# Delta rule: inverse blocks merged by 32x32 products, key lengths from Gram diagonals, decay rows spread through DRAM

## The chip, the cores and the metric

One Trainium2 chip, of which the kernel uses one core. The metric is the device time of one execution in microseconds (us), lower is better. Engines are named as in the profile: PE is TensorE, DVE is VectorE, ACT is ScalarE, POOL is GpSimd; SP is the engine on whose queue all transfers of this kernel are issued (SPq in the profile's rows).

## The reference

A decoder of four layers, each a sequence mixer and an MLP, and a further block behind them, over 16 meta tokens and 256 tokens (T = 272 columns), width 1024, all in float32. Layers 0 and 3 have a gated delta rule as mixer, which is what the change touches. Cut to that:

```python
def gated_deltanet(u, valid, w_in, conv_w, a_log, dt_bias, norm_w, w_out):
    proj = u @ w_in                                   # q, k, v, z, beta, a
    qkv = silu(causal_depthwise_conv(proj[..., :DN_CONV_CH], conv_w))
    q = l2norm(q) * DN_HEAD_K ** -0.5;  k = l2norm(k)  # 8 heads of 128
    beta = sigmoid(beta_logit);  g = -exp(a_log) * softplus(a + dt_bias) * m
    o = chunk_gated_delta_rule(q, k, v, beta, g)
    return (rmsnorm(o, norm_w) * silu(z)) @ w_out

def chunk_gated_delta_rule(q, k, v, beta, g):         # per chunk and head
    gc = cumsum(g)
    decay = exp(where(incl, gc[:, None] - gc[None, :], -inf))
    a_strict = where(strict, (k * beta) @ k.T * decay, 0)
    m = a_strict + eye                                # unit lower triangular
    u = triangular_solve(m, v * beta);  w = triangular_solve(m, k * beta * exp(gc))
    # scan over chunks: v_new = u - w @ state; o = (q*exp(gc)) @ state + (q @ k.T * decay) @ v_new
```

## The kernel before

The residual stream stays on the chip as 128 partitions by 8 by T. Weights come from DRAM in chunks of 1 MB: `chunk` (L405 to L416) issues one load on SP into `wraw` (three buffers), splits it into a high part `whi` (ACT cast, two pieces of 128x1024) and a low part `wlo` (DVE subtraction, four pieces of 128x512, three buffers each). Every product with weights (`mm3`) is three PE products, high by high, high by low and low by high; they show as `pm`. The stages follow one another: delta rule layer 0 (`dn0`, about 6 to 215 us), its MLP, an attention layer, MLP, a recurrent layer, MLP, delta rule layer 3 (`dn3`, about 1050 to 1245 us), and a last block.

In a delta rule layer `_dn` walks through 16 weight chunks in the order k0 k1 v0 q0 k2 v1 q1 k3 z0 v2 q2 v3 q3 z1 z2 z3, each for one pair of heads (four pairs) and each 48 PE products. The load of the next chunk is asked for when the current one begins. The work of the delta rule itself is written as generators that are advanced between the products (`tick`, every 8 products), so it lies in the gaps of the weight products in PE's row of work. A scheduler then fixes one order for each engine and each queue by its own cost model, and each engine works through its list strictly in that order: an instruction that waits holds all behind it, and a transfer on SP that waits for its source or its buffer holds every later load.

The generators that the change touches:
- `dn_gate_cols` (L650 to L702) works out the running sums of the gates and lays them as rows, one of 272 columns per head: PE writes `grow` (8x272), ACT copies it to `rows` in SBUF (L702).
- `dn_ssq` (L742) gives squared lengths of 272 columns for a pair: an ACT square of 128x544 (`sq`), six one-column PE products with ones (`ssq`), a DVE memset and a DVE addition. It is called for the keys (by `dn_keys`) and for the queries (by `dn_chain`).
- `dn_keys` (L755), per pair: for each head PE spreads its row of `rows` over 128 partitions by a product with columns of the identity (`pg`, in PSUM); ACT takes its exponential (`E`, 128x272 per head); DVE subtracts the gate columns under a mask from it (`Dx` 128x128 four times, `Dm` 16x16 twice), ACT exponentiates these. Then key lengths (`kk`, `sk`, `sv`), the Gram products `ga` (four 128x128) and `gm` (two 16x16), and from them DVE forms the triangular matrices `U`.
- `dn_blocks` (L921) inverts all 16x16 diagonal blocks of `U` at once: `U` is written to DRAM (`ud`), read back as 40 blocks (`X`), POOL does the 15 steps, and the result goes through DRAM again (`yd`, `yc`). These four transfers are on SP, between the weight loads, and `yd` waits for POOL.
- `dn_merge` (L947) joins blocks of 16 to blocks of 32, 64 and 128. The step to 32 uses masked full-width operands: DVE builds `uw`, `yf` and `gf` (each 128x512, eight block-diagonal copies under masks), PE does four products of 128x128 by 32 columns for `gp` and eight for `pp`. The later steps use products of single quadrants, 32x32 and 64x64.
- `dn_chain` (L807) runs the recurrence of a pair and needs the list `keys` full and the pair before it solved. Its `kp` products turn the keys and values of the meta tokens.

In the trace each float32 PE product of the delta rule shows as two MATMUL instructions, a transpose as one.

Of the kernel before, what the change touches and what calls it, by code (L numbers as in the profile page):

```python
# [9 lines left out]
F32 = mybir.dt.float32  # L10
F32R = mybir.dt.float32r
AF = mybir.ActivationFunctionType
ALU = mybir.AluOpType
# [127 lines left out]
def _dn_consts():  # L141
    p = np.arange(P)[:, None]
    q = np.arange(P)[None]
    c = np.arange(32)[None]
    comp = (p % 32 >= 16) & (c < 16)
    full = np.concatenate([comp & (p // 32 == b) for b in range(4)], axis=1)
    r = [("mc16", comp), ("mf16", full),
         ("bm32", p // 32 == q // 32), ("in16", p // 16 == np.arange(8)[None]), ("in32", p // 32 == np.arange(4)[None]),
         ("hf16", (p // 16) % 2 == np.arange(2)[None]), ("hf32", (p // 32) % 2 == np.arange(2)[None]),
         ("st16", p % 32 == np.arange(16)[None]), ("mneg", np.where(q >= p, 0.0, -1e30))]  # L150
    return [(n, np.asarray(a, np.float32)) for n, a in r]
# [148 lines left out]
class Prog:  # L300
# [89 lines left out]
    def mm(self, out, lhsT, rhs, start=True, stop=True):  # L390
        self.PE.matmul(out=out, lhsT=lhsT, rhs=rhs, start=start, stop=stop)  # L391
# [238 lines left out]
    def dn_gates(self, s, u, R):  # L630

        d1 = self.d1
        gates = [d1.tile([8, T], F32, name="rows")] + [d1.tile([P, 4, 5], F32, name=n) for n in ("bet", "gc", "ng")]
# [12 lines left out]
    def dn_gate_cols(self, s, gp, R, rows, bet, gc, ng):  # L646
# [55 lines left out]
        self.S.copy(out=rows, in_=rp)  # L702
# [52 lines left out]
    def dn_keys(self, p, kT, gates, ready, keys):  # L755
# [12 lines left out]
        keys += [E, Dx, Dm, sk, sv]  # L768
        for h in range(2):
            pg = self.pst("pg")[:, 0:T]  # L770
            r = 2 * p + h
            mm(pg, self.ident[0:8, r:r + 1].broadcast_to([8, P]), rows)
            act(E[:, h, :], pg, AF.Exp)
            for c in range(2):
                stt(Dx[:, 2 * h + c, :], pg[:, ck[1 + c]], gc[:, p, 2 * h + c:2 * h + c + 1], mneg, ALU.subtract, ALU.min)
            r = RH[h]
            stt(Dm[r], pg[r, 0:16], gc[r, p, 4:5], mneg[0:16, 0:16], ALU.subtract, ALU.min)
# [3 lines left out]
        yield  # L781
        self.dn_ssq(kT, kk)
        act(sk, kk, AF.Sqrt)
        V.reciprocal(out=sv, in_=kk)
        tt(sv, sv, bet[:, p, :], ALU.mult)
# [9 lines left out]
        for h in range(2):  # L795
            mm(gm[RH[h], 0:16], kT[:, h, 0:16], kT[:, h, 0:16])
        for i in range(4):
            stt(U[:, i, :], ga[:, i, :], sv[:, i:i + 1], Dx[:, i, :], ALU.mult, ALU.mult)
# [8 lines left out]
    def dn_chain(self, p, kT, vT, qT, gates, keys, outs, last):  # L807
# [41 lines left out]
        for h in range(2):  # L849
            r = RH[h]  # L850
            self.tr(kp[:, h, :], kT[:, h, ck[1]])
            mm(kp[r, 2, :], kT[:, h, 0:16], self.ident)
            mm(kp[r, 3, :], vT[:, h, 0:16], self.ident)
# [94 lines left out]
    def dn_merge(self, U, yc, Y):  # L948
# [13 lines left out]
        uw = d2.tile([P, 4, P], F32, tag="gf", name="uw", bufs=1)  # L962
        tt(uw, U[:, 0:4, :], bc(dc("bm32"), 1, 4), ALU.mult)
        Ym = d2.tile([48, 48], F32, tag="Ym", name="Ym")
        blocks(Ym.unsqueeze(1), yc[0:48, 4:5, 0, :], dc("in16")[0:48, 0:3], 16, 48, 1)
        yf = d2.tile([P, 4, P], F32, tag="yf16", name="yf", bufs=1)
        blocks(yf, yc[:, 0:4, 0, :], dc("in16"), 16)
# [4 lines left out]
        gp = self.pst("gp")[:, 0:128].rearrange("p (m a) -> p m a", m=4)  # L972
        for m in range(4):
            mm(gp[:, m, :], uw[:, m, :], yw[:, m, 1, :])
        gf = d2.tile([P, 4, P], F32, tag="gf", name="gf", bufs=1)
        gcm = d2.tile([P, 4, 32], F32, tag="gs", name="gcm", bufs=1)
        tt(gf.rearrange("p m (b a) -> p m b a", b=4), bc(gp, 2, 4), bc(dc("mf16").rearrange("p (b a) -> p b a", b=4), 1, 4), ALU.mult)
# [3 lines left out]
        for m in range(4):  # L981
            mm(pp[:, m, 0, :], gf[:, m, :], yw[:, m, 0, :])
            mm(pp[:, m, 1, :], yf[:, m, :], gcm[:, m, :])
# [900 lines left out]
```

## Time and profile before

| | |
|---|---|
| time, median of 3 runs | 2632.33 us |
| runs | 2615.8, 2632.33, 2635.84 us |
| the profiled execution | 2633.17 us |
| its span | 2631.0 us |
| PE busy | 2590.7 us, 98% |
| DVE busy | 2058.9 us, 78% |
| ACT busy | 1474.1 us, 56% |
| POOL busy | 109.5 us, 4% |

The span is what the trace covers; the time of the same execution is 2.17 us longer. The busy shares are means over all stages. The granted clock of PE is given as a part of its full 2.4 GHz, so 0.50 is 1.2 GHz.

### The profile page before, as it was taken

To read this page: it belongs to the slowest core of one execution; us is meant where nothing else is said; L and a number is where in the kernel's file an instruction comes from. 1 tells how busy PE (TensorE), PEld (TensorE's weight loads), DVE (VectorE), ACT (ScalarE), POOL (GpSimd) and SP (SyncE) were. 2 spreads that over 40 slices of the span, in tenths; PEclk is the share of its full clock that TensorE was granted. 3 is DMA by queue.
4 is the path that set the end of the run, shared out by engine and by line. 5 is a ranking of instruction groups with operands and counts; after the bars stand their busy time and mean duration, and the time that the engine had idled before them with its cause. 6 is when DMAs were issued, how large, how long until landed. Compare 5 with 4: busy or idle time off the path is not lost.

```text
span 2631.0 us, 51989 instructions
## 1 busy us (share of the span) xinstructions
PE 2590.7 (98%) x20890; PEld 2512.0 (95%) x20890; DVE 2058.9 (78%) x4637; ACT 1474.1 (56%) x2544; POOL 109.5 (4%) x280
## 2 busy tenths in 40 slices
PE   8999999999999999999999999999999999999998
PEld 8899999899999999989999999999788999999998
DVE  7768967679879976877986877976654987997765
ACT  7777445564457644877645545544544445445544
POOL 1410001000000000330000000000000000000000
PEclk9999999999999999999999999999997999999999
DMA  5226755247545664333875665654213875874553
GB/s 186 95 89 237 276 179 181 99 169 261 194 147 188 259 233 172 98 113 127 313 268 192 241 230 179 217 183 163 81 65 120 286 278 184 312 277 163 177 179 111
DMA packets 89570, 494.56 MB, mean 188 GB/s; under 512 B 18449, under 2 KB 28337, under 8 KB 33265
## 3 DMA queue, kind: packets, MB, share of 16 engines
q1 hardware_dynamic: 89328, 491.23, 53.0%
q8 instruction: 165, 2.70, 0.4%
q14 instruction: 77, 0.62, 0.1%
HBM read 485.23 MB, written 5.96 MB: 187 GB/s over the span
## 4 chain that ended last, share of the span: by engine, by line
PE 92%; DVE 4%; ACT 2%; POOL 1%; issue 1%; DMA 1%; SPq 0%; DVEq 0%; ACTq 0%; POOLq 0%
PE pm L391 81%; PE o L391 1%; PE sp L391 1%; PE ssq L391 1%; PE pp L391 1%; PE go L391 1%; PE ga L391 1%; DVE wlo L415 1%; PE gp L391 1%; PE po L391 1%; POOL yb L938 0%; ACT L358 0%; POOL t L937 0%; ACT whi L412 0%; ACT s L358 0%
## 5 line engine op out<-in xcount | busy, mean ns | idle before, releaser
L391 PE MATMUL pm<-uh,whi 128*128 128x258 f32 (+2 forms) x3768 | 1083.8, 288 | 5.6 <-ACT uh L358 4.0
L391 PE MATMUL pm<-uh,wlo 128*128 128x258 f32 (+2 forms) x3768 | 1086.3, 289 | 0.8 <-DVE wlo L415 0.8
L391 PE MATMUL pm<-ul,whi 128*128 128x258 f32 (+2 forms) x3768 | 1086.2, 289 | 0.3 <-DVE ul L352 0.2
L412 ACT CAST whi<-wraw 128x1024 fp32r<-128x1024 f32 (+1 forms) x767 | 768.4, 1033 | 533.1 <-PE pm L391 306.3
L415 DVE TENSOR_TENSOR wlo<-wraw,whi 128x512 fp32r<-128x512 f32 x1511 | 979.7, 688 | 94.9 <-ACT whi L412 92.4
L391 PEld LDWEIGHTS pm<-uh,whi 128*128 128x128 f32 x3768 | 717.6, 191 | 11.8 <-ACT uh L358 4.4
L391 PEld LDWEIGHTS pm<-uh,wlo 128*128 128x128 f32 x3768 | 717.7, 191 | 8.0 <-issue 4.2
L391 PEld LDWEIGHTS pm<-ul,whi 128*128 128x128 f32 x3768 | 718.0, 191 | 6.4 <-issue 4.2
L391 PE MATMUL pm<-hh,wlo 128*128 128x256 f32 (+1 forms) x1904 | 541.5, 284 | 0.0
L391 PE MATMUL pm<-hh,whi 128*128 128x256 f32 (+1 forms) x1904 | 541.4, 284 | 0.0
L391 PE MATMUL pm<-hl,whi 128*128 128x256 f32 (+1 forms) x1904 | 540.4, 284 | 0.0
L391 PEld LDWEIGHTS pm<-hl,whi 128*128 128x128 f32 x1904 | 361.2, 190 | 0.0
L391 PEld LDWEIGHTS pm<-hh,wlo 128*128 128x128 f32 x1904 | 358.7, 188 | 0.0
L391 PEld LDWEIGHTS pm<-hh,whi 128*128 128x128 f32 x1904 | 358.1, 188 | 0.0
L1375 DVE SCALAR_TENSOR_TENSOR wmod<-wmod,crow 128x1024 f32<-128x1024 f32 x144 | 174.4, 1216 | 0.1
L355 DVE TENSOR_TENSOR h<-h,pm 128x272 f32<-128x272 f32 (+1 forms) x192 | 82.1, 429 | 83.8 <-PE pm L391 83.2
L402 ACT CAST hh<-t 128x256 fp32r<-128x256 f32 x110 | 44.5, 405 | 146.2 <-DVE t L352 146.0
L358 ACT ACT_TABLE_LOAD x90 | 115.5, 1283 | 10.1 <-PE pm L391 4.1
L358 ACT ACTIVATE s<-r 128x272 f32<-128x272 f32 (+1 forms) x128 | 53.7, 425 | 71.1 <-DVE r L352 69.8
L358 ACT ACTIVATE t<-t,b 128x256 f32<-128x256 f32 x110 | 55.5, 506 | 64.0 <-DVE t L355 63.9
L355 DVE TENSOR_TENSOR t<-pm,rstd 128x256 f32<-128x256 f32 x220 | 90.7, 414 | 0.0
L352 DVE SCALAR_TENSOR_TENSOR h<-pm,gate,h 128x256 f32<-128x256 f32 x96 | 46.2, 481 | 50.1 <-PE pm L391 50.0
(456 smaller groups left out, 2847.1 us busy)
## 6 DMA issues: line engine op xcount, KB each, us to landing
wraw<-mlp SPq DMA_DIRECT2D x128, 1024.0 KB, 4.8
wmod<-wmod SPq DMA_DIRECT2D x72, 1024.0 KB, 6.2
wraw<-f1i SPq DMA_DIRECT2D x66, 1024.0 KB, 4.9
wraw<-f2i SPq DMA_DIRECT2D x44, 1024.0 KB, 5.0
wraw<-dnA SPq DMA_DIRECT2D x32, 1024.0 KB, 5.0
wraw<-f1o SPq DMA_DIRECT2D x24, 1024.0 KB, 4.9
wraw<-f2o SPq DMA_DIRECT2D x16, 1024.0 KB, 4.9
wraw<-daA SPq DMA_DIRECT2D x12, 1024.0 KB, 4.9
```

The costliest lines, as they stand in the source:

```text
L352: self.V.scalar_tensor_tensor(out=out, in0=a, scalar=s, in1=b, op0=op0, op1=op1)
L355: self.V.tensor_tensor(out=out, in0=a, in1=b, op=op)
L358: i = self.S.activation(out=out, in_=a, func=func, **k).ins
L391: self.PE.matmul(out=out, lhsT=lhsT, rhs=rhs, start=start, stop=stop)
L402: self.S.copy(out=hi, in_=x)
L412: self.S.copy(out=hi[:, k], in_=raw[:, k])
L415: self.V.tensor_sub(out=lo[:, k], in0=raw[:, k], in1=hi[:, k].bitcast(F32))
L1375: i = self.V.scalar_tensor_tensor(out=junk, in0=w[:, k, :], scalar=1.0, in1=c[:, r, :], op0=ALU.mult, op1=ALU.mult, accum_out=m[:, j:j + 1])
```

## The change

There are three parts, all in the delta rule, so all done for eight pairs of heads in the program (four in each of two layers).

1. `dn_merge`, the step from 16 to 32: `uw`, `yf` and `gf` are no longer built. `gp` is sixteen products of 32x32 on the diagonal quadrants of `U` and `yw`, `pp` is 32 products of 32x32 of `gcm` and `yw`. The constant `mf16` goes.
2. Key lengths: `dn_ssq` is no longer called for keys. DVE multiplies `ga` (four 128x128) and `gm` (two 16x16) by the identity and accumulates along the rows into `kk`. `sk`, `sv` and the list `keys` are therefore filled after the Gram products.
3. Decay rows: ACT copies `grow` to `rs` in SBUF, and a transfer takes it to `rows`, now in DRAM (L703). Per pair one transfer reads two rows into `E` on all 128 partitions (L769; 128x544 float32 is 278 KB); DVE forms `Dx` and `Dm` from `E` in SBUF, and then ACT exponentiates `E` in place, once. The `pg` products go.

Beside these, in `kp` of the first head of a pair, two products with the identity become transposes.

```diff
--- before.py
+++ after.py
@@ -143,8 +143,7 @@
     q = np.arange(P)[None]
     c = np.arange(32)[None]
     comp = (p % 32 >= 16) & (c < 16)
-    full = np.concatenate([comp & (p // 32 == b) for b in range(4)], axis=1)
-    r = [("mc16", comp), ("mf16", full),
+    r = [("mc16", comp),
          ("bm32", p // 32 == q // 32), ("in16", p // 16 == np.arange(8)[None]), ("in32", p // 32 == np.arange(4)[None]),
          ("hf16", (p // 16) % 2 == np.arange(2)[None]), ("hf32", (p // 32) % 2 == np.arange(2)[None]),
          ("st16", p % 32 == np.arange(16)[None]), ("mneg", np.where(q >= p, 0.0, -1e30))]
@@ -630,7 +629,7 @@
     def dn_gates(self, s, u, R):
 
         d1 = self.d1
-        gates = [d1.tile([8, T], F32, name="rows")] + [d1.tile([P, 4, 5], F32, name=n) for n in ("bet", "gc", "ng")]
+        gates = [self.dd.tile([8, T], F32, name="rows")] + [d1.tile([P, 4, 5], F32, name=n) for n in ("bet", "gc", "ng")]
         gw = self.gw if s == 0 else self.chunk(self.A[f"dng{s}"], 512)
         gp = self.pst("gates")
         n = 0
@@ -699,7 +698,9 @@
         for c in range(2):
             o, n = CB[1 + c]
             mm(rp[:, o:o + n], cs[:, 8 * c:8 * c + 8], self.ident)
-        self.S.copy(out=rows, in_=rp)
+        rs = d2.tile([8, T], F32, tag="rr", name="rs", bufs=1)
+        self.S.copy(out=rs, in_=rp)
+        self.nc.sync.dma_start(out=rows, in_=rs)
 
     def proj_out(self, name, ys, N, waits, add):
 
@@ -765,24 +766,17 @@
         Dx = d2.tile([P, 4, P], F32, tag="Dx", name="Dx")
         Dm = d2.tile([48, 16], F32, tag="Dm", name="Dm")
         kk, sk, sv = (d2.tile([P, 5], F32, tag=n, name=n, bufs=4) for n in ("kk", "sk", "sv"))
-        keys += [E, Dx, Dm, sk, sv]
+        self.nc.sync.dma_start(out=E, in_=bass.AP(rows.tensor, rows.offset + 2 * p * T, [[0, P], [1, 2 * T]]))
+        yield 3
         for h in range(2):
-            pg = self.pst("pg")[:, 0:T]
-            r = 2 * p + h
-            mm(pg, self.ident[0:8, r:r + 1].broadcast_to([8, P]), rows)
-            act(E[:, h, :], pg, AF.Exp)
             for c in range(2):
-                stt(Dx[:, 2 * h + c, :], pg[:, ck[1 + c]], gc[:, p, 2 * h + c:2 * h + c + 1], mneg, ALU.subtract, ALU.min)
+                stt(Dx[:, 2 * h + c, :], E[:, h, ck[1 + c]], gc[:, p, 2 * h + c:2 * h + c + 1], mneg, ALU.subtract, ALU.min)
             r = RH[h]
-            stt(Dm[r], pg[r, 0:16], gc[r, p, 4:5], mneg[0:16, 0:16], ALU.subtract, ALU.min)
+            stt(Dm[r], E[r, h, 0:16], gc[r, p, 4:5], mneg[r.start:r.start + 16, r.start:r.start + 16], ALU.subtract, ALU.min)
+        act(E, E, AF.Exp)
         act(Dx, Dx, AF.Exp)
         for r in RH:
             act(Dm[r], Dm[r], AF.Exp)
-        yield
-        self.dn_ssq(kT, kk)
-        act(sk, kk, AF.Sqrt)
-        V.reciprocal(out=sv, in_=kk)
-        tt(sv, sv, bet[:, p, :], ALU.mult)
         yield
         while p > 1 and self.inv[p - 2] is None:
             yield
@@ -794,6 +788,20 @@
             mm(ga[:, 2 * h + c, :], k, k)
         for h in range(2):
             mm(gm[RH[h], 0:16], kT[:, h, 0:16], kT[:, h, 0:16])
+
+        V.memset(kk, 0.0)
+        diag = d2.tile([P, P], F32, tag="dg", name="dg", bufs=1)
+        for i in range(4):
+            V.scalar_tensor_tensor(out=diag, in0=ga[:, i, :], scalar=1.0, in1=self.ident, op0=ALU.mult, op1=ALU.mult,
+                                   accum_out=kk[:, i:i + 1])
+        for r in RH:
+            V.scalar_tensor_tensor(out=diag[r, 0:16], in0=gm[r, 0:16], scalar=1.0, in1=self.ident[r, r], op0=ALU.mult,
+                                   op1=ALU.mult, accum_out=kk[r, 4:5])
+        V.tensor_scalar_add(out=kk, in0=kk, scalar1=EPS)
+        act(sk, kk, AF.Sqrt)
+        V.reciprocal(out=sv, in_=kk)
+        tt(sv, sv, bet[:, p, :], ALU.mult)
+        keys += [E, Dx, Dm, sk, sv]
         for i in range(4):
             stt(U[:, i, :], ga[:, i, :], sv[:, i:i + 1], Dx[:, i, :], ALU.mult, ALU.mult)
         for r in RH:
@@ -849,8 +857,11 @@
         for h in range(2):
             r = RH[h]
             self.tr(kp[:, h, :], kT[:, h, ck[1]])
-            mm(kp[r, 2, :], kT[:, h, 0:16], self.ident)
-            mm(kp[r, 3, :], vT[:, h, 0:16], self.ident)
+            for i, x in ((2, kT), (3, vT)):
+                if h:
+                    mm(kp[r, i, :], x[:, h, 0:16], self.ident)
+                else:
+                    self.tr(kp[r, i, :], x[:, h, 0:16])
         for h in range(2):
             r = RH[h]
             act(ke[:, h, :], kp[:, h, :], AF.Copy, scale=Dx[:, 2 * h, P - 1:P])
@@ -959,28 +970,26 @@
             nb = out.shape[-1] // w
             tt(out.rearrange("p m (b a) -> p m b a", b=nb), bc(y, 2, nb), bc(bc(mask, 1, m), 3, w), ALU.mult)
 
-        uw = d2.tile([P, 4, P], F32, tag="gf", name="uw", bufs=1)
-        tt(uw, U[:, 0:4, :], bc(dc("bm32"), 1, 4), ALU.mult)
         Ym = d2.tile([48, 48], F32, tag="Ym", name="Ym")
         blocks(Ym.unsqueeze(1), yc[0:48, 4:5, 0, :], dc("in16")[0:48, 0:3], 16, 48, 1)
-        yf = d2.tile([P, 4, P], F32, tag="yf16", name="yf", bufs=1)
-        blocks(yf, yc[:, 0:4, 0, :], dc("in16"), 16)
         yw = d2.tile([P, 4, 2, 32], F32, tag="yw", name="yw", bufs=1)
         for t in range(2):
             blocks(yw[:, :, t, :], yc[:, 0:4, t, :], dc("hf16"), 16)
         yield
         gp = self.pst("gp")[:, 0:128].rearrange("p (m a) -> p m a", m=4)
+        b32 = [slice(32 * b, 32 * b + 32) for b in range(4)]
         for m in range(4):
-            mm(gp[:, m, :], uw[:, m, :], yw[:, m, 1, :])
-        gf = d2.tile([P, 4, P], F32, tag="gf", name="gf", bufs=1)
+            for b in b32:
+                mm(gp[b, m, :], U[b, m, b], yw[b, m, 1, :])
         gcm = d2.tile([P, 4, 32], F32, tag="gs", name="gcm", bufs=1)
-        tt(gf.rearrange("p m (b a) -> p m b a", b=4), bc(gp, 2, 4), bc(dc("mf16").rearrange("p (b a) -> p b a", b=4), 1, 4), ALU.mult)
         tt(gcm, gp, bc(dc("mc16"), 1, 4), ALU.mult)
         yield
         pp = self.pst("pp")[:, 0:256].rearrange("p (m t a) -> p m t a", m=4, t=2)
         for m in range(4):
-            mm(pp[:, m, 0, :], gf[:, m, :], yw[:, m, 0, :])
-            mm(pp[:, m, 1, :], yf[:, m, :], gcm[:, m, :])
+            for b in b32:
+                mm(pp[b, m, 0, :], gcm[b, m, :], yw[b, m, 0, :])
+            for b in b32:
+                mm(pp[b, m, 1, :], yw[b, m, 0, :], gcm[b, m, :])
         tt(yw, yw, pp, ALU.subtract)
         blocks(Y, yw[:, :, 0, :], dc("in32"), 32)
         yt = d2.tile([64, 4, 64], F32, tag="yt", name="yt", bufs=1)
```

Counted over the program's instructions: `pg` 16 products to 0, one-column `ssq` products 96 to 48 for the delta rule, products of 128x128 by 32 columns 96 to 0, products of 32x32 in these two steps 0 to 384; DVE `uw`, `yf`, `gf` 8 each to 0, DVE products for `kk` 0 to 48; ACT `E` 16 of 272 columns to 8 of 544, squares of keys 8 to 0; SP gains two transfers for `rows` and eight for `E`.

The order also moves. First SP's queue in layer 0, from the load of chunk k2 on. `wraw<-dnA` are the weight loads, in order k2, v1, q1, k3 and so on; what stands in brackets is what the row waits for. Before:

```order
L409 DMA wraw<-dnA 128x2048 [waits DMAHW2_49,DMAHW5_49,DVE_49,Activation_49]
L409 DMA wraw<-dnA 128x2048 [waits DMAHW3_49,DMAHW6_49,DVE_49,Activation_49]
L409 DMA wraw<-dnA 128x2048 [waits DMAHW4_49,DVE_49,Activation_49]
L925 DMA ud<-U_201 128x5x128 [waits DMAHW0_49,DVE_49]
L927 DMA X<-ud 40x16x16 [waits DMAHW0_49,PE_49]
L925 DMA ud<-U_210 128x5x128 [waits DVE_49]
L409 DMA wraw<-dnA 128x2048 [waits DMAHW5_49,DVE_49,Activation_49]
L927 DMA X<-ud 40x16x16 [waits DMAHW2_49,DMAHW1_49,Pool_49]
```

The first three are the loads of v1, q1 and k3, the fourth is z0. After, the same stretch:

```order
L408 DMA wraw<-dnA 128x2048 [waits DMAHW2_49,DMAHW5_49,DVE_49,Activation_49]
L703 DMA rows<-rs 8x272 [waits DMAHW6_49,Activation_49]
L408 DMA wraw<-dnA 128x2048 [waits DMAHW3_49,DVE_49]
L769 DMA E<-rows 128x544 [waits DMAHW6_49,DMAHW0_49]
L769 DMA E<-rows 128x544
L936 DMA ud<-U_201 128x5x128 [waits DVE_49]
L938 DMA X<-ud 40x16x16 [waits DMAHW2_49,PE_49]
L408 DMA wraw<-dnA 128x2048 [waits DMAHW4_49,DVE_49]
L936 DMA ud<-U_210 128x5x128 [waits DMAHW5_49,DVE_49]
L938 DMA X<-ud 40x16x16 [waits DMAHW5_49,DMAHW3_49,Pool_49]
L953 DMA yd<-yb 40x512 [waits Pool_49]
L408 DMA wraw<-dnA 128x2048 [waits DMAHW0_49,DVE_49,Activation_49]
```

The loads here are v1, q1, k3 and z0: k3 has moved behind `ud` and `X` of pair 0, and z0 behind those of pair 1 and `yd` of pair 0.

Second, DVE's list at the same place, around the low parts of chunk k2 and `U` of pair 0 (`U_201`). Before:

```order
L355 TENSOR_TENSOR sv<-sv,bet 128x5
L553 MEMSET raw 128x3
L355 TENSOR_TENSOR raw<-pm,rstd 128x272
L415 TENSOR_TENSOR wlo<-wraw,whi 128x512 x4
L352 SCALAR_TENSOR_TENSOR U_201<-ga,sv,Dx 128x128 x4
L352 SCALAR_TENSOR_TENSOR U_201<-gm,sv,Dm 16x16 x2
L745 MEMSET ssq_527 128x1
L415 TENSOR_TENSOR wlo<-wraw,whi 128x512 x2
```

All four pieces of k2's low part stand ahead of `U` of pair 0. After (the first two pieces stand further up, ahead of all `Dx`):

```order
L351 SCALAR_TENSOR_TENSOR Dx<-E,gc,dnc 128x128 x2
L351 SCALAR_TENSOR_TENSOR Dm<-E,gc,dnc 16x16
L795 SCALAR_TENSOR_TENSOR dg,kk<-ga,ident 128x128
L351 SCALAR_TENSOR_TENSOR vT<-raw,par,vT 128x272
L351 SCALAR_TENSOR_TENSOR U_201<-ga,sv,Dx 128x128 x4
L351 SCALAR_TENSOR_TENSOR U_201<-gm,sv,Dm 16x16 x2
L795 SCALAR_TENSOR_TENSOR dg,kk<-ga,ident 128x128
L351 SCALAR_TENSOR_TENSOR vT<-raw,par,vT 128x272
L795 SCALAR_TENSOR_TENSOR dg,kk<-gm,ident 16x16 x2
L414 TENSOR_TENSOR wlo<-wraw,whi 128x512
L800 TENSOR_SCALAR kk<-kk 128x5
L414 TENSOR_TENSOR wlo<-wraw,whi 128x512
```

The third and fourth piece of k2's low part now stand behind `U_201` and behind `kk` of pair 1.

Third, SP's queue in layer 3, around the loads of z0, v2 and q2. Before:

```order
L942 DMA yd<-yb 40x512 [waits Pool_49]
L409 DMA wraw<-dnA 128x2048 [waits DMAHW1_49,DVE_49,Activation_49]
L944 DMA yc<-yd 128x5x32 [waits DMAHW2_49,DMAHW0_49]
L942 DMA yd<-yb 40x512 [waits Pool_49]
L409 DMA wraw<-dnA 128x2048 [waits DMAHW4_49,DVE_49,Activation_49]
L944 DMA yc<-yd 128x5x32 [waits DMAHW3_49]
```

The first `yd` is that of pair 0, the second that of pair 1; the load between them is z0, the one behind the second is v2. After:

```order
L953 DMA yd<-yb 40x512 [waits Pool_49]
L408 DMA wraw<-dnA 128x2048 [waits DMAHW1_49,DVE_49,Activation_49]
L955 DMA yc<-yd 128x5x32 [waits DMAHW2_49,DMAHW0_49]
L769 DMA E<-rows 128x544 [waits DMAHW3_49,DVE_49]
L408 DMA wraw<-dnA 128x2048 [waits DVE_49,Activation_49]
L953 DMA yd<-yb 40x512 [waits Pool_49]
L955 DMA yc<-yd 128x5x32 [waits DMAHW5_49]
```

Here the load of v2 stands ahead of pair 1's `yd`, and behind the transfer of `E` for pair 2.

## Rows read from the trace of the kernel before

**Rows 1.** The page: the chain that ended last, by engine.

```profile
PE 92%; DVE 4%; ACT 2%; POOL 1%; issue 1%; DMA 1%; SPq 0%; DVEq 0%; ACTq 0%; POOLq 0%
```

**Rows 2.** Windows: stretch, length, busy by engine (instructions), clock, DMA share, GB/s.

```profile
40.00:60.00 20.00, 19.21 (x127) 17.29 (x127) 14.45 (x48) 15.08 (x25) 6.52 (x20) 0.83 0.34 112
1120.00:1140.00 20.00, 17.03 (x154) 15.34 (x153) 10.13 (x32) 9.29 (x19) 2.18 (x8) 0.83 0.57 185
```

**Rows 3.** Timeline of PE in layer 3: start, length, line, operation, count.

```profile
1075.41 1.18 PE L391 MATMUL pg<-rows,ident 8*128 8x272 f32 x4
1076.52 1.19 PE L391 MATMUL ssq<-ones,sq 128*128 128x1 f32 x12
1077.64 1.16 PE L391 MATMUL ga<-kT 128*128 128x128 f32 x8
```

**Rows 4.** Timeline of PE in layer 0: merge products, and what follows each.

```profile
145.36 1.08 PE L391 MATMUL gp<-yw,uw 128*128 128x32 f32 x8
146.27 0.37 PE L391 MATMUL pm<-uh,whi 128*128 128x272 f32 x1
...
147.74 0.41 PE L391 MATMUL pp<-yw,gf 128*128 128x32 f32 x2
...
149.54 0.70 PE L391 MATMUL ssq<-ones,sq 128*128 128x1 f32 x5
...
154.47 0.59 PE L391 MATMUL gp<-yw,U 32*32 32x32 f32 x16
154.99 0.34 PE L396 MATMUL kp<-ident,kT 128*128 128x128 f32 x1
...
157.17 0.21 PE L391 MATMUL pp<-yw,gs 32*32 32x32 f32 x1
...
157.69 0.40 PE L391 MATMUL pm<-uh,whi 128*128 128x272 f32 x1
```

**Rows 5.** Groups of DVE instructions by shape: busy, mean ns, idle before.

```profile
L355 DVE TENSOR_TENSOR uw<-U,dnc 128x512 f32<-128x512 f32 x8 | 5.6, 700 | 0.0
L1375 DVE DVE_READ_ACCUMULATOR wmod<-wmod,crow 128x1 f32 x144 | 11.8, 82 | 0.0
```

**Rows 6.** Timelines of DVE: the first `U` of layer 0, and `kT` in layer 3.

```profile
43.55 1.12 DVE L352 SCALAR_TENSOR_TENSOR U<-ga,sv,Dx 128x128 f32<-128x128 f32 x4
...
1075.02 0.49 DVE L352 SCALAR_TENSOR_TENSOR kT<-raw,par,kT 128x272 f32<-128x272 f32 x1
```

**Rows 7.** Timelines of ACT (row copy, exponential, cast of q2) and PE, layer 0.

```profile
35.50 0.38 ACT L702 COPY rows<-grow 8x272 f32<-8x272 f32 x1 [0.74 <-PE grow L391]
42.13 0.63 ACT L358 ACTIVATE Dx<-Dx 128x512 f32<-128x512 f32 x1
92.85 1.04 ACT L412 CAST whi<-wraw 128x1024 fp32r<-128x1024 f32 x1
...
43.35 0.43 PE L391 MATMUL pm<-ul,whi 128*128 128x272 f32 x1
43.58 0.43 PE L391 MATMUL pm<-uh,wlo 128*128 128x272 f32 x1
```

**Rows 8.** DMA issues: transfer, queue, count, KB each, us to landing.

```profile
wraw<-dnA SPq DMA_DIRECT2D x32, 1024.0 KB, 5.0
ud<-U SPq DMA_DIRECT2D x8, 320.0 KB, 2.5
```

**Rows 9.** Timeline of SP in layer 0, then of SP and PE in layer 3.

```profile
37.09 0.33 SPq L409 DMA_DIRECT2D wraw<-dnA  x1
...
49.81 0.36 SPq L927 DMA_DIRECT2D X<-ud  x1
...
65.79 0.31 SPq L942 DMA_DIRECT2D yd<-yb  x1
...
1122.54 0.34 SPq L409 DMA_DIRECT2D wraw<-dnA  x1
...
1129.14 0.68 PE L391 MATMUL gp<-yt,U 64*64 64x64 f32 x8 [2.58 <-ACT yt L358]
```

## The prediction

> **What bounds the kernel now.** I read the page first: PE is busy 98% of the span (table above) and holds 92% of the chain that ended last [rows 1]. So instructions taken off PE shorten the time by what they held of it, unless something else makes PE wait. The second view is the table of stretches in the delta rule layers [rows 2]: from 40 to 60 us and from 1120 to 1140 us the granted clock is 0.83, and 20 us at 0.83 lose 3.4 us. The third is the timeline at the one long wait of PE in these layers, 2.58 us before `gp` at 1129.14 [rows 9]. Its cause: SP issued the load of v2 only at 1122.54 [rows 9], for it stood behind pair 1's `yd`, which waits for POOL (third place of the order above). The load came late for ACT's cast, ACT works in order, and `yt`, for which PE waited, was behind that cast.
>
> **The change, part by part.** Each PE price is a distance from start to start.
>
> *Decay rows.* The `pg` products of a pair go: 1075.41 to 1076.52, 1.11 us [rows 3].
>
> *Key lengths.* The one-column products for keys go: 1076.52 to 1077.64, 1.12 us a pair [rows 3].
>
> *Merge.* Before, `gp` held PE from 145.36 to 146.27 (0.91) and `pp` from 147.74 to 149.54 (1.80), together 2.71 us [rows 4]. After, they are 32 and 64 instructions on single quadrants. Two rows price these. In the later 32x32 `gp` step, whose successive products use the same quadrant, 16 instructions took 0.52 us (154.47 to 154.99), 0.0325 each; in the later 32x32 `pp` step, which mostly alternates between two quadrants, 24 took 0.52 (157.17 to 157.69), 0.022 each [rows 4]. The new code goes round four quadrants, so the second row is nearer: 96 x 0.022 = 2.1 us, a gain of 0.6 a pair. By the first row it is 3.1, a loss of 0.4. If four quadrants halve the price once more, it is 1.05, a gain of 1.7.
>
> The Trainium skill bears on this in "TensorEngine Tiling (Array Packing)". Its section Key Properties says that changing the tiling mode drains TensorE. That speaks against this part, which puts small products between full-width ones twice more a pair. The trace has this in its price, for the 0.52 us of [rows 4] run from the first small product to the next full-width one; I add no term. The section Theoretical Speedup gives up to 16 times where both dimensions are 32 or less; that is rival A at its best.
>
> *Transposes in `kp`.* One instruction in place of two; I count nothing.
>
> Sum on PE: 1.11 + 1.12 + 0.6 = 2.83 us a pair, times eight pairs 22.6 us; with the bounds of the merge 14.6 to 31.4.
>
> *DVE and ACT.* DVE loses three products of 128x512 at 0.70 us [rows 5], 2.1 us a pair. It gains four of 128x128 like those of `U`, at 1.12/4 = 0.28 [rows 6], two of 16x16 at no more than that, and six reads of the accumulator at 0.08 [rows 5]: 2.2 at most. So DVE is even. ACT loses one square and one start of an instruction a pair. PE's work covers both except at the places below; uncovered, 1 us a pair would be 8 us.
>
> *The wait at the first pair of layer 0.* The rows now go through DRAM. The copy ends at 35.50 + 0.38 = 35.9 [rows 7]. The write to DRAM is small; by the nearest landing time, 2.5 us for `ud` [rows 8], `rows` is there at 38.4. `E` (278 KB, near `ud` with 320) is issued then, right behind the load of q1 from 37.09 [rows 9], which needs 5.0 us [rows 8], to 42.1. I take 42.5 for the landing of `E`, with 41 (both side by side) and 44 (one after the other) as bounds. DVE waits for it at `Dx`, and in its new list the third and fourth piece of k2's low part stand behind that, behind `U` of pair 0 and `kk` of pair 1 (second place of the order). From 42.5: four `Dx`, two `Dm` and two `vT` rows, 6 x 0.28 + 2 x 0.49 = 2.7 [rows 6]; ACT's exponentials of `E` and `Dx`, 2 x 0.63 = 1.3 [rows 7]; `U` 6 x 0.28 = 1.7, which ends at 48.2; then rows of `kk` and `vT` and the piece itself, about 2.5. The third piece is ready near 50.5. In PE's list 28 products of k2 stand ahead of the first that needs it. Before, k2 began near 43.2, at the low clock with 0.23 us a product (43.35 to 43.58, [rows 7]), so PE was at this place at 43.2 + 28 x 0.23 = 49.6. Now it gets there 0.9 later, though two `pg` steps and one `ssq` step, 3.3 us of the sum, should have been saved by then: 4.2 us are given back. What the clock does is open: a low stretch is here already [rows 2], and one may follow the wait, 3.4 us as in layer 3. I take +5, from 2 to 9.
>
> *Queue, layer 0.* k3's load moves behind `ud` and `X` of pair 0, to 48.2 + 2.5 = 50.7. It lands at 55.7; PE, at k2 from 43.2, has v1 and q1 ahead of k3. POOL took 16.0 us from `X` to `yd` of a pair (49.81 to 65.79, [rows 9]), so z0, now behind pair 0's `yd`, is issued near 67, and v2, behind pair 1's, near 83, and lands at 88. PE was done with k3 only at 92.85, when the cast of q2 could take its buffer [rows 7], and had z0 ahead of v2 still. So nothing is late here, and v2 is nearest to it, by some 8 us.
>
> *Queue, layer 3.* v2's load now stands ahead of pair 1's `yd`, and behind `E` of pair 2, which needs no POOL (third place). So the wait of [rows 9] should go: 2.58 us, and most of the 3.4 us of low clock in this stretch [rows 2], 3.0. I take -5.6, from 0 (still late) to -6.
>
> Sum: -22.6 + 5 - 5.6 = -23.2 us. Against the profiled execution, 2633.17 us (span 2631.0 and 2.17 around it), that gives 2610 us. The median of the runs is 2632.33, 0.84 below that execution; the runs spread over 20 us, almost the whole gain.
>
> **Rivals.** *A: four quadrants overlap, and the first pair's wait is short.* At 0.011 us an instruction the merge gains 1.05 us a pair more, 8.4 us; the wait at its bound of 2 gives 3 more: 2610 - 11.4 = 2599. For it: two quadrants in turn are already cheaper than one. Against it: each small product loads its own weights, and the issue of instructions may bound both rows.
>
> *B: gains are given back at waits.* The order moves in all of both layers, and one late weight load costs 5.6 us. If that of layer 3 stays and one more comes up elsewhere, it is 2610 + 11.2 = 2621; with quadrants at the dear price (1.0 us a pair, 8.2) 2629. For it: five new transfers per layer on the queue of the weights. Against: none waits for POOL, and the loads have some 8 us and more of cover.
>
> *C: slower.* `E` of pairs 2 and 3 waits on SP for DVE to be done with the buffer, and every weight load is behind it. If each of the eight `E` and two `rows` transfers makes one load late, at 5.6 us, it is 2633 - 22.6 + 56 = 2666. It decides from nine such loads on: (22.6 + 26.3)/5.6 is 8.7. Against it: `ud`, `X`, `yd` and `yc` are 32 such transfers in the kernel before, and made one long wait.
>
> That the change does nothing, since its steps lie off the path, I exclude: they are on PE, which is busy 98%.
>
> **How the numbers follow.** Forecast 0.52, A 0.17, B 0.24, C 0.07. A measurement of this kernel can tell about 1%, 26 us, from no change; faster by that is below 2606. The forecast's own range, by the bounds of the merge and of the first wait, is 2600 to 2618, and about 0.22 of its 0.52 lie below 2606. So faster is 0.17 + 0.22 = 0.39, same 0.30 + 0.24 = 0.54, slower 0.07. The range goes from 2597, just under A, to 2630, the dear end of B, and leaves out C and the tails.
>
> **What would show it.** In the profile after: no `pg`, half the delta rule's `ssq` and some 20 us less busy time on PE; `gp` of 32 instructions in about 0.7 us and `pp` of 64 in about 1.4; DVE idle at `Dx` until the transfer lands between 41 and 44 us, and PE waiting for the low part of k2; in layer 3 no wait near 1120, and v2's load ahead of `yd`. The prediction is wrong if small products cost over 0.03 us each, if weight loads are late behind `E`, or if the low clock holds longer than before in these layers.

## The result

The changed kernel is slightly slower: 2640.51 us median of 20 runs against 2621.86 for the kernel before (20 runs), a ratio of 1.0051 with a 95% interval of 1.0031 to 1.0071. The profiled execution took 2643.3 us, its span is 2641.1. The runs of every kernel here fall roughly into two groups some 15 us apart, by the clock of a stretch of the last block near 1960 to 2010 us (last section), and medians and ratios move with the share of each. Ratios come from runs taken side by side and are given with 95% intervals; 0.01 in a ratio is 26 us. Beside them stands the time of the two delta rule layers in the profiled execution, which this stretch doesn't touch, but which is one execution of each kernel.

The page of the changed kernel: busy time by engine, and the chain that ended last (compare [rows 1]).

```profile
PE 2567.0 (97%) x21322; PEld 2491.8 (94%) x21322; DVE 2054.6 (78%) x4709; ACT 1466.0 (56%) x2526; POOL 116.1 (4%) x280
PE 88%; DVE 4%; POOL 3%; DMA 2%; ACT 2%; issue 1%; SPq 0%; POOLq 0%; DVEq 0%; ACTq 0%
```

PE is busy 23.7 us less, as the change means it to be. But PE's part of the chain fell from 92% to 88%, and POOL (1% to 3%) and DMA (1% to 2%) came in. The windows, with the columns of [rows 2], show where:

```profile
40.00:60.00 20.00, 14.38 (x98) 13.78 (x97) 18.13 (x68) 15.37 (x23) 5.61 (x14) 0.83 0.34 109
60.00:80.00 20.00, 13.42 (x112) 12.57 (x110) 11.68 (x33) 10.35 (x21) 14.86 (x44) 0.91 0.25 78
80.00:100.00 20.00, 12.98 (x183) 12.00 (x184) 11.56 (x28) 6.89 (x14) 4.29 (x10) 0.67 0.33 115
...
1120.00:1140.00 20.00, 10.90 (x156) 10.06 (x158) 11.84 (x32) 10.92 (x16) 10.64 (x32) 0.66 0.52 170
```

PE stands still for a third of the time from 40 to 100 us, and for almost half of the stretch in layer 3. Waits of PE of over 0.3 us sum up to 29.0 us in layer 0 (8.8 before) and 16.7 in layer 3 (3.0 before), 33.9 us more. The terms of PE: the `pg` products and half of `ssq` are gone from the trace of after, 1.11 + 1.12 us a pair by [rows 3]; for the merge, from PE's timeline (start, length, count):

```profile
87.02 0.45 PE L390 MATMUL gp<-yw,U 32*32 32x32 f32 x32
87.41 0.39 PE L390 MATMUL pm<-uh,wlo 128*128 128x272 f32 x1
...
88.24 0.26 PE L390 MATMUL pp<-yw,gcm 32*32 32x32 f32 x8
...
88.92 0.39 PE L390 MATMUL pm<-ul,whi 128*128 128x272 f32 x1
```

0.39 us for 32 and 0.68 for 64 instructions, 1.07 us in place of 2.71 [rows 4]: 1.64 a pair. That is 3.87 us a pair and 31 us in all. The layers as a whole, from the last addition to `h` ahead of them (the start, for layer 0) to the first behind their recurrence, took 8.5 us (layer 0) and 1.1 us (layer 3) more than before, 404.6 us together against 395.0, 9.6 of the 10.1 us by which the spans differ. (These sums are "the layers" below.) So 31.0 us were saved, 33.9 went into waits, and about 7 remain, which I put down to the low clock behind the waits. That part is a remainder, but the clock fell in both layers: its mean is 0.91 in layer 0 and 0.94 in layer 3, against 0.96 and 0.98 before.

**The first wait** is the one that was foreseen. Timelines of SP, DVE and PE:

```profile
36.10 2.54 SPq L769 DMA_DIRECT2D E<-rows  x2
...
42.50 0.61 DVE L351 SCALAR_TENSOR_TENSOR Dx<-E,gc,dnc 128x128 f32<-128x128 f32 x2 [0.76 <-DMA E<-rows]
...
50.22 0.69 DVE L414 TENSOR_TENSOR wlo<-wraw,whi 128x512 fp32r<-128x512 f32 x1
...
50.96 0.59 PE L390 MATMUL pm<-uh,wlo 128*128 128x272 f32 x1 [4.68 <-DVE wlo L414]
```

DVE itself stood idle for `E` for only 0.76 us. The rest of PE's wait of 4.7 us comes from the order: the third piece of k2's low part stands behind `Dx`, `U`, `kk` and rows of `vT`, which took DVE from 42.5 to 50.2.

**The second** was not. Timelines of SP, ACT, DVE and PE around 80 us:

```profile
54.04 0.37 SPq L936 DMA_DIRECT2D ud<-U  x1
67.15 0.30 SPq L938 DMA_DIRECT2D X<-ud  x1
68.83 0.30 SPq L953 DMA_DIRECT2D yd<-yb  x1
69.24 0.36 SPq L408 DMA_DIRECT2D wraw<-dnA  x1
70.64 0.39 SPq L955 DMA_DIRECT2D yc<-yd  x1
71.08 0.51 SPq L769 DMA_DIRECT2D E<-rows  x1
...
74.18 1.04 ACT L411 CAST whi<-wraw 128x1024 fp32r<-128x1024 f32 x1 [7.82 <-DMA wraw<-dnA]
75.68 0.68 DVE L351 SCALAR_TENSOR_TENSOR Dx<-E,gc,dnc 128x128 f32<-128x128 f32 x2 [6.89 <-DMA E<-rows]
...
80.07 1.34 DVE L414 TENSOR_TENSOR wlo<-wraw,whi 128x512 fp32r<-128x512 f32 x2
80.81 0.60 PE L390 MATMUL pm<-uh,wlo 128*128 128x272 f32 x1 [7.38 <-DVE wlo L414]
```

SP stands still from 54.4 to 67.15: `X` of pair 1 has one buffer, which POOL is still reading for pair 0. Behind it come `yd` of pair 0, which waits for POOL too, then the load of z0, and only at 71.08 `E` of pair 2. DVE reaches `Dx` of pair 2 at 68.8 and waits for that transfer; the low part of k3, whose weights had long landed, stands behind it on DVE, and PE waits for that.

**The third** is the load of v2 behind `yd` of pair 1, with the cast on ACT in between:

```profile
84.42 0.31 SPq L953 DMA_DIRECT2D yd<-yb  x1
84.84 0.33 SPq L408 DMA_DIRECT2D wraw<-dnA  x1
...
91.11 1.99 ACT L411 CAST whi<-wraw 128x1024 fp32r<-128x1024 f32 x2 [10.10 <-DMA wraw<-dnA]
95.52 0.50 DVE L351 SCALAR_TENSOR_TENSOR qT<-raw,par,qT 128x272 f32<-128x272 f32 x1 [6.47 <-ACT qT L357]
...
96.41 0.87 PE L390 MATMUL gp<-yw,U 32*32 32x32 f32 x16 [6.22 <-DVE yw L354]
```

PE did not need v2 yet. But ACT, in order, held the `qT` copies behind v2's cast, DVE held `yw` behind `qT`, and the merge on PE needed `yw`.

**Layer 3** (compare [rows 9]) has the second wait again:

```profile
1117.18 0.30 SPq L953 DMA_DIRECT2D yd<-yb  x1
...
1119.42 0.47 SPq L769 DMA_DIRECT2D E<-rows  x1
1119.98 0.38 SPq L408 DMA_DIRECT2D wraw<-dnA  x1
...
1126.36 0.82 DVE L351 SCALAR_TENSOR_TENSOR Dx<-E,gc,dnc 128x128 f32<-128x128 f32 x2 [10.23 <-DMA E<-rows]
...
1128.85 0.60 PE L390 MATMUL pm<-uh,whi 128*128 128x272 f32 x1 [10.28 <-DVE raw L354]
```

The load of v2 at 1119.98 now is ahead of pair 1's `yd` and the wait of before is gone, as forecast. A wait of 10.3 us on `E`, which stands behind pair 0's `yd`, is there in its place.

### The profile page after: what moved, and what is told of

Same layout as the page of the kernel before. It is cut to its first block, busy times and chain, and to the rows that moved or that the text cites. A ratio compares the mean times of both kernels' runs of the same rounds, so it can differ in the third digit from the quotient of the medians.

```text
span 2641.1 us, 52934 instructions
## 1 busy us (share of the span) xinstructions
PE 2567.0 (97%) x21322; PEld 2491.8 (94%) x21322; DVE 2054.6 (78%) x4709; ACT 1466.0 (56%) x2526; POOL 116.1 (4%) x280
## 4 chain that ended last, share of the span: by engine, by line
PE 88%; DVE 4%; POOL 3%; DMA 2%; ACT 2%; issue 1%; SPq 0%; POOLq 0%; DVEq 0%; ACTq 0%
PE pm L390 79%; POOL t L948 1%; PE o L390 1%; POOL yb L949 1%; PE sp L390 1%; PE go L390 1%; DVE wlo L414 1%; PE ssq L390 1%; DMA E<-rows 1%; PE po L390 0%; ACT L357 0%; DMA ud<-U 0%; PE pp L390 0%; PE ga L390 0%; ACT s L357 0%
## 5 line engine op out<-in xcount | busy, mean ns | idle before, releaser
L390 PEld LDWEIGHTS pm<-uh,whi 128*128 128x128 f32 x3768 | 718.8, 191 | 19.6 <-DVE raw L354 10.9
L357 ACT ACTIVATE t<-t,b 128x256 f32<-128x256 f32 x110 | 55.5, 506 | 64.2 <-DVE t L354 64.1
L390 PE MATMUL pm<-yh,whi 128*128 128x272 f32 (+1 forms) x288 | 83.1, 291 | 2.5 <-ACT yh L401 1.8
```

The lines of the kernel that those rows point to most:

```text
L357: i = self.S.activation(out=out, in_=a, func=func, **k).ins
```

## The experiments

The theory in its first form (W): the loss comes with the transfers of `E`. Rivals: any part moves the order, and the order is what is slow (O); the small products between full-width ones pull the granted clock down (D).

**The merge alone.** The change's edits in `dn_merge` and `kp`, in the kernel before:

```diff
-            mm(gp[:, m, :], uw[:, m, :], yw[:, m, 1, :])
+            for b in b32:
+                mm(gp[b, m, :], U[b, m, b], yw[b, m, 1, :])
```

> The kernel before with the merge on quadrants and the two transposes alone; lengths and decay rows as before. In the profile of the changed kernel 32 small instructions of gp held PE 0.39 us and 64 of pp 0.68, against 0.91 and 1.80 before: 1.64 us a pair, 13 us over eight pairs. Theory W (the loss comes from the transfers of E on the queue of the weights): no new wait here, so 11 to 17 us faster than before. Rival O (any of the three parts moves the order, and the new order is what is slow): faster by less than 5 us or slower, with new waits of PE of 4 us and more in the delta rule layers. Rival D (small products between full-width ones pull the granted clock down): PE's waits as before, but the clock in the delta rule stretches lower than before and the gain under 7 us.

Measured: ratio 0.9972 (0.9946 to 0.9999), 7 us faster (layers: 389.6 us, 5.4 less than before). So about half of the 13 us came through, though the interval, 0 to 14 us, doesn't exclude all of it. Its longest wait, which is new, lies in layer 3; timelines of SP, DVE and PE:

```profile
1117.86 0.29 SPq L944 DMA_DIRECT2D yd<-yb  x1
...
1123.86 0.20 DVE L354 TENSOR_TENSOR Ym<-yc,dnc 48x48 f32<-48x48 f32 x1 [9.58 <-DMA yc<-yd]
...
1125.63 0.87 PE L390 MATMUL gp<-yw,U 32*32 32x32 f32 x16 [9.40 <-DVE yw L354]
```

Here DVE itself has come to the merge of pair 1 and waits for POOL's result; the merge of pair 0 on PE needs `yw`, which is behind it. The clock speaks against D: its mean in the two layers is 0.97 and 0.95 (0.96 and 0.98 before), low only in layer 3, where the wait is.

**The key lengths alone.** `dn_ssq(kT, kk)` out, diagonals of `ga` and `gm` in:

```diff
-        self.dn_ssq(kT, kk)
+            V.scalar_tensor_tensor(out=diag, in0=ga[:, i, :], scalar=1.0, in1=self.ident, op0=ALU.mult, op1=ALU.mult,
+                                   accum_out=kk[:, i:i + 1])
```

> The kernel before with the key lengths from the diagonals of the Gram products alone; merge and decay rows as before. PE loses 1.12 us a pair, 9 us in all. Theory W: 6 to 10 us faster, no wait of over 4 us that was not there before. Rival O: the lengths come later (after ga), U and with it all of the inverse later by the DVE rows in between, 2 to 3 us; loads behind yd on the queue get late and it is slower by 3 us or more.

Measured: 1.0026 (1.0003 to 1.0050), 7 us slower (layers: 400.3 us, 5.3 more than before), though PE does 9 us less. Timelines of SP, ACT and PE show the shape of the third wait above, with no transfer of `E` in the kernel:

```profile
83.20 0.30 SPq L950 DMA_DIRECT2D yd<-yb  x1
84.95 0.36 SPq L952 DMA_DIRECT2D yc<-yd  x1
85.42 10.01 SPq L409 DMA_DIRECT2D wraw<-dnA  x2
...
90.39 1.04 ACT L412 CAST whi<-wraw 128x1024 fp32r<-128x1024 f32 x1 [13.52 <-DMA wraw<-dnA]
...
93.05 0.59 PE L391 MATMUL pm<-uh,wlo 128*128 128x272 f32 x1 [10.86 <-DVE wlo L415]
```

**The decay rows alone.**

```diff
-            mm(pg, self.ident[0:8, r:r + 1].broadcast_to([8, P]), rows)
-            act(E[:, h, :], pg, AF.Exp)
+        self.nc.sync.dma_start(out=E, in_=bass.AP(rows.tensor, rows.offset + 2 * p * T, [[0, P], [1, 2 * T]]))
```

> The kernel before with the decay rows through DRAM alone; merge and lengths as before. PE loses 1.11 us a pair, 9 us in all. Theory W: slower than before by 10 to 30 us; in both delta rule layers DVE waits at Dx of the third pair for E, 5 us or more, because E stands on the queue behind yd or yc of the first pair, which waits for POOL, and PE waits behind it for the low part of a chunk. Rival O: within 6 us of before, since no single part is to blame.

Measured: 1.0078 (1.0052 to 1.0103), 20 us slower. DVE waited 5.2 us for `E` of pair 2 at 72.6 and 4.7 at 1123.9, and PE 3.8 and 5.1 us behind that; and the cast of q2 waited 9.2 us for its load, which stood behind pair 1's `yd`, PE 6.3 behind it. By the ratios the dearest part, as W has it, but two fifths of these waits are not for `E`, and the layers took 400.6 us, 5.6 more than before and about as much as with the lengths alone. The profiled span is 16.5 us longer than before, and the other 10.9 us lie outside the layers and are not traced here.

**Merge and lengths, without the rows.** The edits of the first two together.

> The changed kernel without its decay rows part (pg as in the kernel before). PE loses 1.64 + 1.12 us a pair, 22 us in all. Theory W: 16 to 26 us faster than before, and so 30 or more faster than the changed kernel. Rival O: less than 8 us faster than before, with waits of PE in the delta rule layers.

Measured: 1.0014 (0.9989 to 1.0040), level with before (layers: 397.4 us, 2.4 more), where 22 us came off PE. PE waited 8.9 us at 92.2 and 7.5 at 1138.6, each behind a cast that waited for a load, which stood behind pair 1's `yd`. So W in its first form falls, and O's forecast came true: without any `E` the gain goes as well. What the waits of all four have in common is POOL, either through SP's queue, in which loads stand behind `X`, `yd` and `yc`, or straight, where DVE waits for `yc`. Theory Q is the first, P the second; both say that PE, with less work, gets to these places sooner and finds POOL not done.

**`yd` and `yc` off SP, in the changed kernel.**

```diff
-        q.dma_start(out=yd, in_=yb)
+        self.nc.gpsimd.dma_start(out=yd, in_=yb)
```

and the same for `yc`.

> The changed kernel with the transfers yd and yc issued by POOL instead of SP, so that neither weight loads nor E stand behind POOL's inversion; ud, X and E stay on SP. Theory Q (the queue hands the gain back): the loads of z0 and v2 and E of the third pair go out some 8 us earlier, the waits of PE of 7.4 and 6.2 us in layer 0 and 10.3 us in layer 3 go, 15 to 30 us faster than the changed kernel. Theory P (POOL's two inversions in a row, 16 us each, are themselves what the rest waits for, in DVE at Ym and yw of the merge): the loads are early, but PE waits as long as before at the merge; within 8 us of the changed kernel.

Measured: 0.9937 (0.9913 to 0.9962), 2611.5 us median, 30 us less than the changed kernel by the ratios, and 17 less than the kernel before. Not all of this can be laid to the edit: the layers took 388.2 us, 16.4 less than in the changed kernel and 6.8 less than before, and most of the rest lies in the stretch of the last block, where this profile has a clock of 1.00 (1960 to 2000 us) and that of the changed kernel 0.86 and 0.50. The wait at 96 us is gone. Not so the second one. SP and PE:

```profile
53.94 0.37 SPq L936 DMA_DIRECT2D ud<-U  x1
68.66 0.30 SPq L938 DMA_DIRECT2D X<-ud  x1
69.06 0.40 SPq L408 DMA_DIRECT2D wraw<-dnA  x1
69.56 0.37 SPq L769 DMA_DIRECT2D E<-rows  x1
...
80.41 0.59 PE L390 MATMUL pm<-uh,wlo 128*128 128x272 f32 x1 [7.17 <-DVE wlo L414]
```

`X` of pair 1, and with it all behind it, still waits for POOL to be done with its only buffer.

**The same edit in the merge alone.**

> The kernel before with the merge part alone, and yd and yc issued by POOL. The merge alone was 7 us faster than before, with a wait of PE of 9.4 us in layer 3 behind DVE waiting for yc of the second pair. Theory Q: this wait shrinks to under 3 us and the time is 15 us or more below the kernel before. Theory P: a wait of 7 us or more stays in layer 3 at the merge of the second pair, the time is within 5 us of the merge alone.

Measured: 1.0000 (0.9974 to 1.0025; layers: 390.8 us, 1.2 more than without the edit). P holds here: DVE waited 9.2 us for `yc` at 1120.3, PE 9.1 behind it. The queue was not what this kernel waited for.

**The same edit in the kernel before**, as a control.

> Control: the kernel before with yd and yc issued by POOL, the same edit that made the changed kernel 29 us faster. The kernel before had one wait of PE behind this queue (2.6 us, with up to 3.4 us of low clock behind it). Theory Q (the change brings PE to the waits sooner, and only then does the queue hold it): 0 to 8 us faster than the kernel before. If it gains 15 us or more, the queue held back the kernel before just as much, and the change is not what made it matter; if it is slower, the transfers of POOL's own queue cost something by themselves.

Measured: 1.0032 (1.0007 to 1.0056), 8 us slower (layers: 402.3 us, 7.3 more than before), with waits of PE of 3.6 and 2.9 us at the merge. The edit is no gain by itself; in the layers it is worth 16 us where the change has brought PE to the queue sooner. (Two buffers for `X`, as below, don't fit into the kernel before: its pool would need 61.1 KB per partition and has 60.2. So this control covers the first of the two queue edits alone.)

**POOL's work halved, in both kernels.**

```diff
-        for k in range(15, 0, -1):
+        for k in range(15, 7, -1):
```

> The changed kernel with the first 8 of POOL's 15 inversion steps alone (the other 7 are left out, so the blocks are not fully inverted); POOL takes some 8 us less per pair. All queues as in the changed kernel. Theories Q and P alike: what waits for POOL comes 8 us earlier for the first pair and 16 for the second, the waits of PE of 7.4, 6.2 and 10.3 us go or fall to 2 us, 20 to 35 us faster than the changed kernel. Rival E (the transfer of E itself, or the low clock, costs the time): less than 8 us faster.

> The kernel before with the first 8 of POOL's 15 inversion steps alone (the other 7 left out). Control for the run above: in the kernel before PE waited once, 2.6 us, with 3.4 us of low clock behind it. Theories Q and P: 0 to 8 us faster than the kernel before, far less than the changed kernel gains by the same edit. Rival E: about as much as the changed kernel gains by it.

Measured: 0.9917 (0.9884 to 0.9949) for the changed kernel and 0.9964 (0.9938 to 0.9990) for the one before. So it is worth 35 us in the one and 9 in the other (layers: 377.1 us, 27.5 less, and 389.5, 5.5 less). The waits at 80, 96 and 1128 us became 3.0, 1.5 and 4.2 us. Rival E, which had the two gains alike and the first under 8 us, falls.

**Two buffers for `X` as well**, in the changed kernel with `yd` and `yc` on POOL.

```diff
-        X = d2.tile([40, 16, 16], F32, tag="X", name="X", bufs=1)
+        X = d2.tile([40, 16, 16], F32, tag="XX", name="X", bufs=2)
```

> The changed kernel with yd and yc issued by POOL and two buffers for X instead of one. With yd on POOL alone (2611.5 us) SP still stood still for 15 us in each layer: X of the second pair waits until POOL has read the first one's buffer, and the load of z0 and E of the third pair stand behind it (issued at 69.1 and 69.6 us; PE waited 7.2 us at 80.4 and 8.4 us at 1115). Theory Q (what stands on SP behind POOL is late): with two buffers nothing on SP waits for POOL in the first half of a layer, both waits go, 8 to 16 us less again, 2595 to 2604 us. Theory P (POOL's inversion itself is what is waited for): the waits move to the merge, less than 4 us gained.

Measured: 0.9926 (0.9899 to 0.9953), the fastest ratio of a kernel that does all the work, 33 us under the changed kernel, but only 3 less than with one buffer, which is less than the intervals tell apart. In the layers, at 379.8 us, it is 8.4 less than with one buffer, within Q's 8 to 16, and 24.8 less than in the changed kernel; the ratios hide it, since this kernel's profile has the last block's low stretch (0.51 from 1960 to 1980 us) and that of the kernel with one buffer has not. The mechanism went as Q says. Timeline of SP, and of DVE and PE at one of the waits that are left:

```profile
54.41 0.37 SPq L936 DMA_DIRECT2D ud<-U  x1
58.13 0.29 SPq L938 DMA_DIRECT2D X<-ud  x1
59.81 0.33 SPq L408 DMA_DIRECT2D wraw<-dnA  x1
64.10 0.32 SPq L769 DMA_DIRECT2D E<-rows  x1
...
162.84 0.20 DVE L354 TENSOR_TENSOR Ym<-yc,dnc 48x48 f32<-48x48 f32 x1 [6.33 <-DMA yc<-yd]
...
165.81 1.22 PE L390 MATMUL ksp<-St,kT 128*128 128x128 f32 x4 [5.20 <-ACT St L884]
```

`E` goes out at 64.1 in place of 71.1, and the waits at 80 and 1115 us are gone. What is left of PE's long waits is the first one (4.3 us) and two later in the layers, 5.2 us at 165.8 and 3.9 at 1189.0; and from 80 to 100 us the clock is at 0.66. Those two are what P describes: ahead of them DVE waited 6.3 and 4.7 us for `yc`, POOL's result, with rows behind it that ACT and PE needed.

**All transfers of `E` at the front**, `X`, `yd` and `yc` on SP as in the changed kernel.

```diff
+        self.Es = [d2.tile([P, 2, T], F32, tag="E", name="E", bufs=4) for _ in range(4)]
+        for p, E in enumerate(self.Es):
+            self.nc.sync.dma_start(out=E, in_=bass.AP(rows.tensor, rows.offset + 2 * p * T, [[0, P], [1, 2 * T]]))
```

> The changed kernel with all four transfers of E of a layer issued directly behind rows, with four buffers; X, yd and yc on SP as in the changed kernel. Theory Q in its narrow form (it is E of the third pair that is late, and DVE waits for it): the waits of 7.4 us (80.8) and 10.3 us (1128.9) go, the one of 6.2 us (96.4, load of v2) stays; 10 to 20 us faster than the changed kernel. Wide form (the weight loads behind X and yd would hold ACT just as long): under 8 us faster.

Measured: 1.0014 (0.9982 to 1.0046), 10 us under the changed kernel, between what the two forms gave, but with intervals that overlap. In the profiled execution, the longest of the twelve, the layers took 405.8 us, 1.2 more than in the changed kernel, as in the wide form. The waits for `E` are gone. In their place PE waited 4.6 us at 84.5 behind the cast of v2, and in both layers behind that of q2, whose load stands behind pair 1's `yd`; ACT and PE at these two:

```profile
94.87 1.05 ACT L411 CAST whi<-wraw 128x1024 fp32r<-128x1024 f32 x1 [9.12 <-DMA wraw<-dnA]
96.55 1.11 PE L390 MATMUL gp<-yt,U 64*64 64x64 f32 x8 [7.02 <-ACT yt L357]
...
1143.00 1.05 ACT L411 CAST whi<-wraw 128x1024 fp32r<-128x1024 f32 x1 [12.55 <-DMA wraw<-dnA]
1144.68 1.11 PE L390 MATMUL gp<-yt,U 64*64 64x64 f32 x8 [12.34 <-ACT yt L357]
```

**Merge and lengths with both queue edits**, without the rows.

> The changed kernel without its decay rows part (pg as before), with yd and yc issued by POOL and two buffers for X. Without the queue edit this was level with the kernel before, with waits of PE of 8.9 and 7.5 us behind the load of v2 and of q2. Theory Q: both go, and the 22 us taken off PE come through: 2600 to 2612 us. Theory P: waits of 7 us and more stay at the merge, 2620 us or more.

Measured: 0.9955 (0.9924 to 0.9987), 15 us less than without the queue edits (layers: 386.8 us, 10.6 less). The waits behind v2 and q2 are gone, so the queue held this one too. But of the 22 us taken off PE only 12 came through by the ratio and 8.2 in the layers, and the median, 2619.97 us, lies where P's range begins: waits of PE of 2.8 us at 125 and of 5.1 and 3.4 us in layer 3 are there, and ahead of each DVE waited for `yc` (8.3, 9.1 and 3.6 us). Behind the queue comes POOL itself.

## Why the prediction was wrong

Forecast was 2610 us, with 0.39 for faster and 0.07 for slower by over 1%; it is 0.5% slower, which the prediction counts as the same (0.54), but lies above its range of 2597 to 2630 us. (The forecast's own range of 2600 to 2618 doesn't follow from its bounds: with the merge 8.8 us better and the first wait at 2 it is 2598, with the merge 8 worse and the wait at 9 it is 2622. The measured time is above either.)

- *The terms of PE*: `pg` and `ssq` went as forecast. The merge was taken at a gain of 0.6 us a pair and gained 1.64; the size of rival A was the right one. The sum on PE was 31 us, not 22.6.
- *The first wait*: right in its mechanism and its size, with some luck in between: `E` was issued at 36.1, 2.3 us sooner than forecast, and took 6.4 us to land where 4.1 were forecast, and the two cancel. `E` was there at 42.5 (42.5 forecast), the third piece of k2 came at 50.2 and was done by 50.9 (50.5), PE waited for it at 51.0.
- *Queue, layer 0*: this step failed, "So nothing is late here". The issue times were near (z0 at 69.2 for 67, v2 at 84.8 for 83); when they were due was wrong, in two ways. It asked when PE would need a chunk. But ACT and DVE come to a chunk far ahead of PE, with other work behind it that PE needs at once: v2 was due when ACT got to its cast, at 81 us, not when PE gets to v2. That was the mechanism of the one wait of before, which the prediction had described, and then left out of the rule for the loads. And of the transfers of `E` only the first pair's was priced as a wait for DVE. `E` of pair 2 was looked at as something that might hold loads, not as something that is itself held. (The 92.85 us that it took for PE's end of k3 is when ACT, in order, came to the cast of q2 right behind a copy; k3 may have been done before.)
- *Queue, layer 3*: the wait of before went, and `E` brought a longer one, 10.3 us for 2.6. "`E` of pair 2, which needs no POOL" is true of the transfer and false of its place: `X` and `yd`, which need POOL, are ahead of it on the same queue.
- *Rival B* had the right mechanism, at the wrong price: two late places at 5.6 us. There were three at 6 to 10, and smaller ones. What was said against it, "none waits for POOL", was the same mistake.
- *What no step had*: POOL's chain as a bound on PE. The prediction used POOL's 16 us to time the loads, and never asked what PE does when it comes there sooner. In both kernels the way from `U` of pair 0 to `yd` of pair 1 is two inversions of some 16 us each and their transfers (in layer 0 from `ud` at 45.1 to `yd` at 84.4 before, from 48.6 to 84.4 after). Before, PE's work filled this time almost to the end, with one wait of 2.6 us left. Most of what was taken off PE inside it became waiting. Halving POOL's steps in both kernels shows it (35 us against 9, in the layers 27.5 against 5.5), and the waits for `yc` that are left when the queue is out of the way agree.
- *Of its own signs of being wrong* the clock came true: it was lower than before in both layers. Loads were late too, but behind `yd`, not behind `E`.

The Trainium skill, in "DMA: Bandwidth & Descriptors", section "Anatomy of one DMA — SWDGE (gpsimd) path", says that a semaphore wait of a transfer happens on the sequencer that issues it, ahead of the dispatch. The trace agrees: SP issued nothing between 54.4 and 67.15 us while `X` waited. By that rule each row of the queue has to be read with the longest wait of all rows ahead of it; the prediction had the order and the waits in view and priced each row by its own.

## What to carry to other kernels

Before a term is counted as saved, follow the serial chain of the slow engine through the same stretch (here POOL: two times 16 us); work taken off the busy engine inside it turns into a wait once that chain is longer. On a queue and on an engine in order, a row is due when the first engine comes to what hangs on it, not when the last one needs it, and it inherits the waits of every row ahead of it. Here transfers that wait for a slow engine did better on that engine's own queue, with two buffers for what they fill: with both edits the change is 15 us faster than before in the layers, where without them it is 9.6 slower. Such an edit is to be tried together with the change that makes it matter, since alone it may cost (8 us in the kernel before).

## What the runs showed of the hardware

Products on four quadrants in turn cost half of what the nearest row of before, two quadrants in turn at 22 ns, gave: 0.39 us for 32 instructions, 12 ns each, and 0.68 for 64, 10.6 ns, up to the start of the next full-width product. The Trainium skill, in "TensorE: Matmul & The Clock Gate", section "Wait — 56ns, not 53.3ns?", has 25 ns as the least distance between two products, however small; on single quadrants in turn the trace shows less than half of that, and the measurement decides.

One stretch of the last block, which no edit here touches, runs at either level of the clock. Windows of the kernel before, and of the one with the key lengths alone, whose profiled execution took 2621.78 us (median of its runs 2642.61):

```profile
1980.00:2000.00 20.00, 20.00 (x97) 18.42 (x96) 4.54 (x10) 6.54 (x8) 0.00 (x0) 0.57 0.09 27
```

```profile
1980.00:2000.00 20.00, 20.00 (x155) 18.44 (x155) 10.06 (x20) 8.92 (x11) 0.00 (x0) 1.00 0.31 106
```

PE is busy throughout in both, at 0.57 of the clock in one and at 1.00 in the other, and 1960 to 1980 us is alike (0.58 and 1.00): 17 us between two executions of the same stretch of work, if PE bounds it. The spans agree: outside the two delta rule layers the one took 2235.9 us and the other 2219.2. What decides which it is, no run here shows.
